# Two-layer encoder trunk: paired token tiles after the mixer, stores issued by POOL, rows reloaded later, an end that runs row by row

## The chip, the cores and the metric

The kernel runs on one core of a Trainium2 chip. Five engines work from streams of their own, each strictly in its own order, and wait for one another by semaphores: TensorE (PE, with its weight loads shown as PEld), VectorE (DVE), ScalarE (ACT), GpSimd (POOL) and SyncE (SP, which here only issues DMAs). The metric is device time in microseconds; less is better.

## What is computed

```python
def _layer_norm(x, g, b): ...          # mean and variance of each row of 1024

def _swiglu(x, w_gate, w_up, w_down):
    g = jnp.einsum('bsd,df->bsf', x, w_gate)
    u = jnp.einsum('bsd,df->bsf', x, w_up)
    return jnp.einsum('bsf,fd->bsd', jax.nn.silu(g) * u, w_down)

def reference(x, ...):
    for layer in range(2):             # layer 0: MLA and sliding window; layer 1: FoX and chunked
        mix = ...                      # attention heads, then one output projection
        x = _layer_norm(DEEPNORM_ALPHA * x + mix, ln1_g[layer], ln1_b[layer])
        ffn = _swiglu(x, ffn_w_gate[layer], ffn_w_up[layer], ffn_w_down[layer])
        x = _layer_norm(DEEPNORM_ALPHA * x + ffn, ln2_g[layer], ln2_b[layer])
    return x
```

x has 1024 tokens of 1024 numbers in float32; the hidden width D_FF is 2816.

## The kernel before

**Precision.** Every float32 operand is split in two fp32r halves: ACT casts the high half (line 105), DVE subtracts to get the low half (line 106), and a product is three matmuls for each 128-deep step (`mm3`, line 127). What is called a split below is this pair of operations. A transposed operand comes from `turn_block`: four 128x128 transposes on PE into one bank of PSUM, then a split out of that bank.

**Stages.** For each layer: the mixer (projections, attention), the late half of the output projection with the first LayerNorm, `gate_up`, `down`, the second LayerNorm. Both FFN products are done by a scheme with seven products of half-size blocks in place of eight (Strassen's), so blocks of the operands are first added to one another.

**Late output projection and LN1.** `out_proj` (line 605) goes over the eight token tiles of 128 rows, 24 matmuls each; DVE adds each half into the row tile (line 619), then `ln_pipe` (line 178) is pushed: statistics on DVE (153, 155), small operations on POOL (144, 146), scale (DVE 193 or 200 with help of ACT 163 and POOL 164), the add of b on DVE (200), the store of the row to `xr_scr` on SP (1269), and `turn_sums` (line 242). For tiles 0 to 3 the row's two halves are transposed at once into the blocks b11 and b21. For tiles 4 to 7 `sums` needs row tt-4 and row tt: it forms four differences t1 to t4 (DVE 252) in two `s` tiles and turns five blocks (PE 235); these are put on a list `later` and run after the last row.

**gate_up** (line 282). 22 steps f (2816 / 128), in pairs. A step is seven products of 12 matmuls, 84 in all, with weights that DVE sums (288, 289) and splits. Its results are combined on DVE and ACT in `t` tiles (365 to 395). The hidden values and their sums, seven to a pair, are stored to HBM (336), as are four sums of the down weights (329), by SP. The first four steps start with one product each, the **heads**, that needs b11 and b21 only (24 matmuls, line 127), and can run while the sums are being made.

**down** (line 420). For each half of the tokens, products over 11 steps j: a1 x b1 and so on, named by their operands (a11·b11, s1·t1, a12·b21, ..., s2·t2, s3·t3, a22·t4), all for four row tiles in four banks. `parts` loads two halves of an operand with SP (430, 431) and splits them (ACT, DVE). The saved rows come back from `xr_scr` (456) and are scaled by ACT (457). Rows 0 to 3 are complete after s2·t2, rows 4 to 7 after a22·t4, the last product; each complete row is pushed into the second LayerNorm, which in layer 0 stores to `x_scr` (SP, 1279) and turns the row for layer 1 (PE 172), and in layer 1 stores the output (1275). s1·t1, s3·t3 and others use the two `pt` banks as accumulators, the same two banks into which `turn_block` turns.

**What sets the order.** The functions are written in program order, several as generators, and a tile framework places each instruction in its engine's stream: program order gives the priority, the pools of tiles (`gp`, `tp` and so on in CFG, number of buffers) decide when a buffer is free. Once placed, each stream is fixed. All DMAs before go out from SP, on one hardware queue.

Of the kernel before, what the change touches and what calls it, by code (L numbers as in the profile page):

```python
# [32 lines left out]
CFG = dict(gp=30, wrp=3, whp=6, sp=3, hp=6, bp=2, tp=11, pd=3, ps=2, pt=2, pv=1)  # L33
# [6 lines left out]
class Core:  # L40
# [137 lines left out]
    def ln_pipe(self, y, g, b, turn, done):  # L178
# [5 lines left out]
        def push(tt):
            if 0 <= tt - 1 < n:
                self.ln_scale(y[tt - 1], st[tt - 1], g)
            if tt < TT:
                st[tt] = self.ln_stats(y[tt])
            if n <= tt < TT:
                mv, r = st[tt]  # L190
                for op, s, row in ((ALU.subtract, mv[:, 0:1], g), (ALU.mult, r, b)):
                    for o in (slice(0, 512), slice(512, D)):
                        nc.vector.scalar_tensor_tensor(y[tt][:, o], y[tt][:, o], s, row[:, o], op0=op,  # L193
                                                       op1=ALU.mult if row is g else ALU.add)
                        if row is b:
                            done(tt, y[tt][:, o], o)
            z = tt - 2
            if 0 <= z < TT:
                if z < n:
                    nc.vector.tensor_tensor(y[z], y[z], b, op=ALU.add)  # L200
                    done(z, y[z])
                if turn is not None:
                    turn(z)
# [78 lines left out]
    def gate_up(self, xb, wgu, ops, later):  # L282
# [3 lines left out]
        heads = 4  # L286
# [30 lines left out]
        def down_sums(j):  # L317
# [103 lines left out]
    def down(self, y, xr_scr, ops, lng, lnb, turn_next, done):  # L421
# [5 lines left out]
        def parts(j, a, b, homes=None):  # L427
# [4 lines left out]
            if homes is None:  # L432
                h, l = (self.w().rearrange("p s c -> p (s c)") for _ in range(2))
            else:
                h, l = next(homes), next(homes)
# [941 lines left out]
```

## Time and profile before

| | us |
|---|---|
| median of 3 runs | 2542.03 (2538.09 to 2548.68) |
| the profiled execution, as timed | 2547.79 |
| its span in the trace | 2546.0 |
| PE busy | 2381.7 (94%) |
| DVE busy | 1657.1 (65%) |
| ACT busy | 1123.6 (44%) |
| POOL busy | 598.0 (23%) |

Stages in the trace: mixer of layer 0 to about 449 us, its late projection and LN1 to 510, gate_up with its heads to 958, down to 1217; the same for layer 1 to 1785, 1870, 2300 and 2524; the last rows are done at 2546. Read first the busy tenths of PE in 40 slices of 63.65 us: where a slice is not at 9, PE is waiting, and the windows, the timeline and the waits of that place say for whom. The granted clock (PEclk) says whether a matmul ran at full speed.

### The profile page before, as it was taken

To read this page: it belongs to the slowest core of one execution; us is meant where nothing else is said; L and a number is where in the kernel's file an instruction comes from. 1 tells how busy PE (TensorE), PEld (TensorE's weight loads), DVE (VectorE), ACT (ScalarE), POOL (GpSimd) and SP (SyncE) were. 2 spreads that over 40 slices of the span, in tenths; PEclk is the share of its full clock that TensorE was granted. 3 is DMA by queue.
4 is the path that set the end of the run, shared out by engine and by line. 5 is a ranking of instruction groups with operands and counts; after the bars stand their busy time and mean duration, and the time that the engine had idled before them with its cause. 6 is when DMAs were issued, how large, how long until landed. Compare 5 with 4: busy or idle time off the path is not lost.

```text
span 2546.0 us, 35845 instructions
## 1 busy us (share of the span) xinstructions
PE 2381.7 (94%) x11912; PEld 1988.3 (78%) x11912; DVE 1657.1 (65%) x3566; ACT 1123.6 (44%) x2292; POOL 598.0 (23%) x966
## 2 busy tenths in 40 slices
PE   8998999889999999969899999999879999999996
PEld 7977887667888887858688888878758788887885
DVE  3577756868677764566546565656768677764567
ACT  5476756342323325334346665554442232324342
POOL 3532455500000000021344654354600000000012
PEclk9999999989999999979899999999979999999998
DMA  4235232325454469314121212141325544459632
GB/s 155 87 101 158 76 112 65 124 83 180 161 162 157 158 231 360 106 61 176 63 79 42 71 44 63 44 147 53 132 80 176 166 154 161 170 169 378 209 110 86
DMA packets 190906, 337.88 MB, mean 133 GB/s; under 512 B 22392, under 2 KB 48376, under 8 KB 190720
## 3 DMA queue, kind: packets, MB, share of 16 engines
q1 hardware_dynamic: 190720, 335.58, 40.1%
q8 instruction: 95, 1.56, 0.3%
q14 instruction: 91, 0.75, 0.1%
HBM read 236.89 MB, written 94.40 MB: 130 GB/s over the span
## 4 chain that ended last, share of the span: by engine, by line
PE 73%; DVE 12%; DMA 7%; ACT 4%; issue 3%; POOL 2%; SPq 1%; DVEq 0%; ACTq 0%; POOLq 0%
PE pd L127 42%; PE ps L127 12%; PE pt L127 7%; PE pv L689 3%; PE pt L678 3%; PE pv L127 2%; DMA wr<-in_wgu 2%; DVE g L106 2%; DMA g<-in_wd 1%; DVE wh L106 1%; DVE s L650 1%; DVE g L200 1%; PE ps L718 1%; DVE g L193 1%; PE ps L719 1%
## 5 line engine op out<-in xcount | busy, mean ns | idle before, releaser
L127 PE MATMUL pd<-g,wh 128*128 128x512 f32 (+1 forms) x2940 | 738.9, 400 | 31.6 <-ACT g L105 8.1
L127 PEld LDWEIGHTS pd<-g,wh 128*128 128x128 f32 (+1 forms) x2940 | 546.7, 190 | 159.0 <-ACT g L105 9.7
L144 POOL TENSOR_SCALAR m<-m 128x1 f32<-128x1 f32 x32 | 16.8, 525 | 1294.8 <-DVE m L155 1293.3
L106 DVE TENSOR_TENSOR wh<-g,wh 128x1024 fp32r<-128x1024 f32 x138 | 173.3, 1260 | 163.7 <-ACT wh L105 148.8
L105 ACT CAST g<-s 128x512 fp32r<-128x512 f32 x192 | 116.7, 621 | 334.7 <-PE pd L127 147.8
L105 ACT CAST wh<-g 128x1024 fp32r<-128x1024 f32 x138 | 145.0, 1053 | 199.6 <-PE pt L127 63.7
L105 ACT CAST h<-pt 128x512 fp32r<-128x512 f32 (+3 forms) x350 | 157.9, 464 | 138.2 <-PE pt L678 122.4
L106 DVE TENSOR_TENSOR h<-pt,h 128x512 fp32r<-128x512 f32 (+2 forms) x334 | 177.5, 538 | 62.9 <-ACT h L105 60.7
L127 PE MATMUL ps<-g,g 128*128 128x512 f32 (+3 forms) x816 | 201.5, 382 | 8.4 <-DMA g<-kr_scr 4.9
L660 POOL TENSOR_SCALAR s<-s,m 128x128 f32<-128x128 f32 (+1 forms) x192 | 138.3, 722 | 232.1 <-DVE m L659 176.9
L127 PEld LDWEIGHTS ps<-g,g 128*128 128x128 f32 x816 | 147.5, 191 | 37.6 <-DVE m L650 7.3
L127 PE MATMUL pd<-g,g 128*128 128x512 f32 (+2 forms) x756 | 174.4, 376 | 2.2 <-ACT g L105 1.1
L116 POOL TENSOR_TENSOR wh<-wr,wh 128x512 fp32r<-128x512 f32 (+4 forms) x113 | 138.8, 1236 | 150.7 <-ACT wh L115 100.6
L655 ACT ACTIVATE s<-s,m 128x128 f32<-128x128 f32 (+1 forms) x192 | 144.1, 751 | 60.5 <-DVE m L653 50.9
L689 PE MATMUL pv<-h,g 128*128 128x256 f32 x928 | 161.6, 295 | 6.2 <-ACT h L105 2.5
L127 PEld LDWEIGHTS pd<-g,g 128*128 128x128 f32 x756 | 137.2, 190 | 26.0 <-ACT g L105 1.9
L127 PE MATMUL pd<-wh,g 128*128 128x256 f32 (+2 forms) x1056 | 154.1, 294 | 0.0
L106 DVE TENSOR_TENSOR g<-s,g 128x512 fp32r<-128x512 f32 x192 | 131.8, 700 | 33.1 <-ACT g L105 31.0
L689 PEld LDWEIGHTS pv<-h,g 128*128 128x128 f32 x928 | 130.0, 190 | 18.4 <-ACT h L105 7.3
L127 PEld LDWEIGHTS pd<-wh,g 128*128 128x128 f32 x1056 | 142.1, 193 | 1.9 <-DVE g L106 0.3
L678 PE MATMUL pt<-ident,s 128*128 128x128 f32 x816 | 134.0, 276 | 7.2 <-POOL s L660 2.7
L127 PE MATMUL pt<-g,g 128*128 128x512 f32 x528 | 135.0, 393 | 3.5 <-DVE t L383 3.0
(235 smaller groups left out, 4388.1 us busy)
## 6 DMA issues: line engine op xcount, KB each, us to landing
wr<-in_wgu SPq DMA_DIRECT2D x192, 256.0 KB, 2.7
g<-in_wd SPq DMA_DIRECT2D x154, 256.0 KB, 4.1
t<-g SPq DMA_DIRECT2D x88, 256.0 KB, 2.0
s<-t SPq DMA_DIRECT2D x88, 256.0 KB, 2.8
g<-s SPq DMA_DIRECT2D x88, 256.0 KB, 4.5
g<-t SPq DMA_DIRECT2D x88, 256.0 KB, 5.2
a<-t SPq DMA_DIRECT2D x66, 256.0 KB, 2.4
g<-a SPq DMA_DIRECT2D x66, 256.0 KB, 5.3
```

What stands on the lines that cost most here:

```text
L105: self.nc.scalar.copy(hi, src)
L106: self.nc.vector.tensor_tensor(lo, src, fv(hi), op=ALU.subtract)
L116: self.nc.gpsimd.tensor_tensor(hl[:, 1, :], raw, fv(hl[:, 0, :]), op=ALU.subtract)
L127: self.nc.tensor.matmul(out, stat[a], mov[c], start=first and i == 0, stop=last and i == 2, skip_group_check=more)
L193: nc.vector.scalar_tensor_tensor(y[tt][:, o], y[tt][:, o], s, row[:, o], op0=op, op1=ALU.mult if row is g else ALU.add)
L200: nc.vector.tensor_tensor(y[z], y[z], b, op=ALU.add)
L650: nc.vector.tensor_tensor_reduce(out=sb[:, x:y], in0=p, in1=in1, scale=1.0, scalar=m0, op0=ALU.add, op1=ALU.max, accum_out=m)
L655: nc.scalar.activation(sb[:, 0:w], sb[:, 0:w], AF.Exp, bias=neg, scale=scale, accum_out=sm)
L660: nc.gpsimd.tensor_scalar(sb[:, 0:w], sb[:, 0:w], rc, 1.0, op0=ALU.mult, op1=ALU.mult)
L678: nc.tensor.transpose(tp[:, (kb - b0) * P : (kb - b0) * P + P], sb[:, (kb - k0) * P : (kb - k0) * P + P], self.ident)
L689: nc.tensor.matmul(pv, vt(kb), pair[kb // 4][l][:, kb % 4, :], start=c == 0, stop=c == 2 * (last + 1 - first) - 1)
L718: nc.tensor.matmul(p, qt[:, q], kt[:, c : c + w], start=True, stop=False)
```

## The change

Six things are done together.

- The late output projection and LN1 take the tiles in the order 0, 4, 1, 5, 2, 6, 3, 7, so that both rows of a pair are there when the second is; `sums` of tiles 4, 5 and 6 run at once, only that of 7 is put off. The differences stand in four `t` tiles in place of two `s` tiles. There are three heads in place of four.
- The stores of gate_up (336, 329), of `xr_scr` and of `x_scr` are issued by POOL in place of SP: 121 in each layer's gate_up, 10 to each `xr_scr`, 10 to `x_scr`, 272 in all. The output's stores stay on SP.
- In `down` the reload of the rows and their scaling stand after the second product instead of the first.
- Rows 0 to 3 are pushed into LN2 after s3·t3 has been written down instead of after s2·t2.
- In the last product seven of eleven j go as in the other products, all four rows for each j; the four j that are left are kept in tiles and run row by row, so that the four rows end 12 matmuls apart.
- Pools: gp 30 to 31, tp 11 to 9; six of the late projection's weights come from the `wh` pool.

```diff
-CFG = dict(gp=30, wrp=3, whp=6, sp=3, hp=6, bp=2, tp=11, pd=3, ps=2, pt=2, pv=1)
+CFG = dict(gp=31, wrp=3, whp=6, sp=3, hp=6, bp=2, tp=9, pd=3, ps=2, pt=2, pv=1)
...
-    def ln_pipe(self, y, g, b, turn, done):
+    def ln_pipe(self, y, g, b, turn, done, order=range(TT)):
...
         def sums(tt):
             a, b = slice(0, 512), slice(512, D)
             x, z = y[tt - 4], y[tt]
-            ta, tb = self.s(), self.s()
-            t1, t2, t3, t4 = ta[:, a], ta[:, b], tb[:, a], tb[:, b]
+            t1, t2, t3, t4 = (self.t() for _ in range(4))
...
                 self.turn_block(xb, "b21", y[tt][:, 512:D], tt)
+            elif tt < TT - 1:
+                sums(tt)
             else:
                 later.append(lambda: sums(tt))
...
-        heads = 4
+        heads = 3
...
             for n, t in ((b11, "t1"), (b12, "t3"), (b22, "t2"), (b21, "t4")):
-                nc.sync.dma_start(o[n], t)
+                nc.gpsimd.dma_start(o[n], t)
...
-            put = lambda n, t: nc.sync.dma_start(o[n], t)
+            put = lambda n, t: nc.gpsimd.dma_start(o[n], t)
...
-        for tt in range(TT):
-            y[tt] = self.g(F32)
-            nc.sync.dma_start(y[tt], xr_scr[tt * P : tt * P + P, :])
-            nc.scalar.mul(y[tt], y[tt], ALPHA)
         us = [self.s() for _ in range(2)]
...
         product(pb, "s1", "t1")
+        for tt in range(TT):
+            y[tt] = self.g(F32)
+            nc.sync.dma_start(y[tt], xr_scr[tt * P : tt * P + P, :])
+            nc.scalar.mul(y[tt], y[tt], ALPHA)
...
             add(y[mt][:, hi], u[mt], y[mt][:, hi])
+        pb = bank_b()
+        kept = 4
+        homes = iter([self.h() for _ in range(6)] + [self.s().bitcast(F32R), self.g()])
+        product(pb, "s3", "t3")
+        last = [parts(j, "a22", "t4", homes) for j in range(n - kept, n)]
+        for mt in range(4):
             push(mt)
-        pb = bank_b()
-        product(pb, "s3", "t3")
         for mt in range(4):
             add(u[mt], pb[mt], u[mt])
...
-        last = [parts(j, "a22", "t4", homes) for j in range(n)]
         pa = bank_a()
+        product(pa, "a22", "t4", m=n - kept)
         for mt in range(4):
-            for j in range(n):
-                mms(pa[mt], last[j], mt, j == 0, j == n - 1)
+            for j in range(kept):
+                mms(pa[mt], last[j], mt, False, j == kept - 1)
             add(y[4 + mt][:, lo], pa[mt], y[4 + mt][:, lo])
             push(4 + mt)
...
-            late_ws.extend(c.out_weights(wo, late, 0, 5, c.g))
+            late_ws.extend(c.out_weights(wo, late, 0, 1, c.g) + c.out_weights(wo, late, 1, 5, c.wflat))
...
+        order = (0, 4, 1, 5, 2, 6, 3, 7)
```

**PE at the end of layer 0's LN1.** Before; line 127 is a matmul (the `pd` tile 6734 is the fourth head), line 235 a transpose of a turn; `s` tiles are sums, `g` tiles rows.

```order
L127 MATMUL pd_6734<-g_6008,wh_6731 128x512
L235 MATMUL pt_6615<-ident,s_6584 128x128 x4
L235 MATMUL pt_6625<-ident,s_6584 128x128 x4
L235 MATMUL pt_6675<-ident,g_4833 128x128 x4
L235 MATMUL pt_6685<-ident,s_6673 128x128 x4
L235 MATMUL pt_6695<-ident,s_6673 128x128 x4
L235 MATMUL pt_6705<-ident,s_6674 128x128 x4
L235 MATMUL pt_6715<-ident,s_6674 128x128 x4
L235 MATMUL pt_6765<-ident,g_4834 128x128 x4
L235 MATMUL pt_6775<-ident,s_6763 128x128 x4
L235 MATMUL pt_6785<-ident,s_6763 128x128 x4
L127 MATMUL pd_6899<-g_6494,g_6822 128x512
```

The same engine and place after the change; line 240 is the turn's transpose, line 130 the matmul, `pd` 6623, 6662 and 6701 are the three heads.

```order
L240 MATMUL pt_6424<-ident,g_4833 128x128 x4
L240 MATMUL pt_6434<-ident,t_6420 128x128 x4
L240 MATMUL pt_6444<-ident,t_6421 128x128 x4
L240 MATMUL pt_6454<-ident,t_6422 128x128 x4
L240 MATMUL pt_6464<-ident,t_6423 128x128 x4
L240 MATMUL pt_6473<-ident,g_4830 128x128 x4
L240 MATMUL pt_6482<-ident,g_4830 128x128 x4
L130 MATMUL pd_6623<-g_5994,wh_6615 128x512
L130 MATMUL pd_6662<-g_5994,wh_6654 128x512
L130 MATMUL pd_6701<-g_5994,wh_6693 128x512
```

Before, ten turns of sums follow the last head; after, all heads follow the turns (sixteen turns stand in a row ahead of them), and of the sums only those of tile 7 come later.

**ACT at the end of layer 0's gate_up.** Before; line 457 scales a reloaded row, 105 is the cast of the next product's operand, 371 and 394 belong to the last step f.

```order
L371 ACTIVATE t_9900<-pd_9859 128x512
L457 ACTIVATE g_10202<-g_10202 128x1024
L457 ACTIVATE g_10205<-g_10205 128x1024
L457 ACTIVATE g_10208<-g_10208 128x1024
L457 ACTIVATE g_10211<-g_10211 128x1024
L457 ACTIVATE g_10214<-g_10214 128x1024
L394 ACTIVATE t_9872<-t_9872 128x512
L457 ACTIVATE g_10217<-g_10217 128x1024
L105 CAST wh_10053<-g_10050 128x1024
```

After; the lines are 377, 400, 108 and 465.

```order
L377 ACTIVATE t_9904<-pd_9863 128x512
L400 ACTIVATE t_9876<-t_9876 128x512
L108 CAST wh_10057<-g_10054 128x1024
L108 CAST wh_10076<-g_10073 128x1024
L108 CAST wh_10095<-g_10092 128x1024
L108 CAST wh_10114<-g_10111 128x1024
L108 CAST wh_10133<-g_10130 128x1024
L108 CAST wh_10152<-g_10149 128x1024
L465 ACTIVATE g_10421<-g_10421 128x1024
L465 ACTIVATE g_10424<-g_10424 128x1024
```

The row scalings have moved from ahead of the operand casts of a11·b11 to behind six more of them.

**PE around s2·t2 and s3·t3 of layer 0.** Before; `pv` 10878 is a bank of s2·t2, line 172 turns rows 0 and 1, `ps` 11200 and 11201 with `pt` 11202 and 11203 are the banks of s3·t3.

```order
L127 MATMUL pv_10878<-wh_11072,wh_11073 128x512
L172 MATMUL pt_11147<-ident,g_10202 128x128 x4
L172 MATMUL pt_11156<-ident,g_10202 128x128 x4
L172 MATMUL pt_11182<-ident,g_10205 128x128 x4
L172 MATMUL pt_11191<-ident,g_10205 128x128 x4
L127 MATMUL ps_11200<-wh_11207 128x512
```

After; `pt` 11103 is a bank of s3·t3, line 175 turns rows 0 to 2, `pd` 11457 is a bank of the last product.

```order
L130 MATMUL pt_11103<-wh_11306,wh_11305 128x512
L130 MATMUL pt_11103<-wh_11305,wh_11306 128x512
L175 MATMUL pt_11394<-ident,g_10421 128x128 x4
L175 MATMUL pt_11403<-ident,g_10421 128x128 x4
L175 MATMUL pt_11427<-ident,g_10424 128x128 x4
L175 MATMUL pt_11436<-ident,g_10424 128x128 x4
L175 MATMUL pt_11622<-ident,g_10427 128x128 x4
L175 MATMUL pt_11631<-ident,g_10427 128x128 x4
L130 MATMUL pd_11457<-wh_11464 128x512
```

The first turns of layer 1's rows stand one product later, and six of them in place of four are in a row.

## Rows read from the trace of the kernel before

**Rows 1.** The page, parts 1 and 2: busy us, share, instructions; busy tenths by slice.

```profile
PE 2381.7 (94%) x11912; PEld 1988.3 (78%) x11912; DVE 1657.1 (65%) x3566; ACT 1123.6 (44%) x2292; POOL 598.0 (23%) x966
...
PE   8998999889999999969899999999879999999996
```

**Rows 2.** Windows: start:end, us, then PE, PEld, DVE, ACT, POOL busy, PEclk, DMA share, GB/s.

```profile
600.00:900.00 300.00, 294.89 (x1291) 243.15 (x1291) 221.96 (x354) 90.81 (x155) 0.00 (x0) 0.99 0.50 162
```

**Rows 3.** Windows around LN1 of layer 0 and of layer 1, columns as in rows 2.

```profile
452.00:506.00 54.00, 46.10 (x202) 36.16 (x201) 48.58 (x82) 18.06 (x32) 30.86 (x26) 0.91 0.36 127
506.00:551.00 45.00, 33.75 (x160) 26.91 (x158) 26.91 (x56) 20.43 (x49) 1.69 (x2) 0.84 0.20 65
...
600.00:650.00 50.00, 44.89 (x188) 36.06 (x188) 37.74 (x61) 12.30 (x21) 0.00 (x0) 0.97 0.58 189
...
1870.00:1900.00 30.00, 20.70 (x102) 16.35 (x101) 18.57 (x42) 13.69 (x36) 0.00 (x0) 0.80 0.06 18
```

**Rows 4.** Groups of PE by line from 506 to 551: busy us, mean ns | idle before.

```profile
L127 PE MATMUL pd<-g,wh 128*128 128x512 f32 x86 | 22.5, 418 | 3.3 <-ACT t L371 2.8 <-ACT t L365 0.6
L235 PE MATMUL pt<-ident,s 128*128 128x128 f32 x56 | 9.9, 327 | 5.5 <-DVE g L106 4.0 <-DVE h L106 1.4
```

**Rows 5.** Timeline of ACT and of PE after gate_up: start, us, operation [idle before <-releaser].

```profile
962.21 1.06 ACT L457 ACTIVATE g<-g 128x1024 f32<-128x1024 f32 x1 [2.00 <-DMA g<-xr_scr]
...
970.39 1.03 ACT L105 CAST wh<-g 128x1024 fp32r<-128x1024 f32 x1
...
971.48 0.97 PE L127 MATMUL pd<-wh 128*128 128x512 f32 x3 [2.12 <-ACT wh L105]
...
2319.55 0.73 PE L127 MATMUL pd<-wh 128*128 128x512 f32 x2 [2.92 <-ACT wh L105]
```

**Rows 6.** Windows at the same two places, columns as in rows 2.

```profile
950.00:975.00 25.00, 21.63 (x88) 16.48 (x87) 12.22 (x16) 14.04 (x16) 0.00 (x0) 0.96 0.91 342
...
2300.00:2325.00 25.00, 20.83 (x82) 15.76 (x81) 13.45 (x17) 14.80 (x17) 0.00 (x0) 0.93 0.95 361
```

**Rows 7.** Timeline of PE around LN2 of layer 0, columns as in rows 5.

```profile
1130.40 1.97 PE L172 MATMUL pt<-ident,g 128*128 128x128 f32 x8 [15.08 <-DVE g L200]
1134.98 1.09 PE L172 MATMUL pt<-ident,g 128*128 128x128 f32 x4 [2.61 <-DVE g L106]
1138.27 1.09 PE L172 MATMUL pt<-ident,g 128*128 128x128 f32 x4 [2.20 <-DVE g L106]
1142.53 1.22 PE L127 MATMUL ps<-wh 128*128 128x512 f32 x2 [3.17 <-ACT wh L105]
```

**Rows 8.** Windows around LN2 of layer 0, columns as in rows 2.

```profile
1100.00:1150.00 50.00, 26.94 (x107) 21.37 (x106) 34.11 (x42) 15.03 (x20) 14.10 (x12) 0.73 0.30 111
1200.00:1250.00 50.00, 40.93 (x169) 29.97 (x168) 28.14 (x47) 12.91 (x27) 19.52 (x20) 0.83 0.24 80
```

**Rows 9.** Timeline of DVE from 1127 and of POOL from 1124, columns as in rows 5.

```profile
1127.00 6.64 DVE L200 TENSOR_TENSOR g<-g,b 128x1024 f32<-128x1024 f32 x2
...
1138.04 1.22 DVE L200 TENSOR_TENSOR g<-g,b 128x1024 f32<-128x1024 f32 x1
1139.17 0.42 DVE L106 TENSOR_TENSOR g<-pt,g 128x256 fp32r<-128x256 f32 x1
...
1124.62 11.23 POOL L164 TENSOR_TENSOR g<-g,b 128x1024 f32<-128x1024 f32 x4
```

**Rows 10.** Timeline of DVE at the end of the kernel, columns as in rows 5.

```profile
2522.94 1.29 DVE L425 TENSOR_TENSOR g<-pd,g 128x512 f32<-128x512 f32 x2 [7.79 <-PE pd L127]
...
2530.11 9.56 DVE L193 SCALAR_TENSOR_TENSOR g<-g,m,b 128x512 f32<-128x512 f32 x8
2539.59 2.35 DVE L200 TENSOR_TENSOR g<-g,b 128x1024 f32<-128x1024 f32 x2
```

**Rows 11.** SP's waits: engine line <- for whom: us, times, longest.

```profile
SPq L329 <- DVE g L289: 107.0, 88, 4.0
...
SPq L1279 <- DVE g L200: 81.3, 3, 79.8
```

More of the change, by code (lines that the diff above doesn't have):

```diff
@@ L182, in ln_pipe, with push @@
         n = TT - 2
[L184 to L190, printed above, removed]
+        at = dict(enumerate(order))
+        def push(i):
+            if 0 <= i - 1 < n:
+                self.ln_scale(y[at[i - 1]], st[i - 1], g)
+            if i < TT:
+                st[i] = self.ln_stats(y[at[i]])
+            if n <= i < TT:
+                mv, r = st[i]
+                yt = y[at[i]]
                 for op, s, row in ((ALU.subtract, mv[:, 0:1], g), (ALU.mult, r, b)):
                     for o in (slice(0, 512), slice(512, D)):
-                        nc.vector.scalar_tensor_tensor(y[tt][:, o], y[tt][:, o], s, row[:, o], op0=op,
+                        nc.vector.scalar_tensor_tensor(yt[:, o], yt[:, o], s, row[:, o], op0=op,
                                                        op1=ALU.mult if row is g else ALU.add)
                         if row is b:
-                            done(tt, y[tt][:, o], o)
-            z = tt - 2
+                            done(at[i], yt[:, o], o)
+            z = i - 2
             if 0 <= z < TT:
                 if z < n:
-                    nc.vector.tensor_tensor(y[z], y[z], b, op=ALU.add)
-                    done(z, y[z])
+                    nc.vector.tensor_tensor(y[at[z]], y[at[z]], b, op=ALU.add)
+                    done(at[z], y[at[z]])
                 if turn is not None:
-                    turn(z)
+                    turn(at[z])
         return push
@@ L431, in parts @@
             nc.sync.dma_start(raw[:, hi], ops[j][b])
[L432 to L435, printed above, removed]
+            h, l = (next(homes) if homes else self.wflat() for _ in range(2))
             self.split(h, l, raw)
@@ L442, in mms, with product @@
             self.mm3(p, (h[:, c], l[:, c]), (h[:, hi], l[:, hi]), first, last, more)
-        def product(p, a, b, first=True):
-            for j in range(n):
+        def product(p, a, b, first=True, m=n):
+            for j in range(m):
                 op = parts(j, a, b)
@@ L595, in out_weights, with out_proj @@
         return ws
-    def out_proj(self, o_scr, x_src, ws, kts, y, push=None, more=None):
+    def out_proj(self, o_scr, x_src, ws, kts, y, push=None, more=None, order=tuple(range(TT))):
         nc = self.nc
         load = lambda tt: self.weight(o_scr[tt, :, kts[0] : kts[-1] + 1, :].rearrange("p k c -> p (k c)"), 512)
-        nxt = load(0)
+        nxt = load(order[0])
         if more is not None:
             ws = ws + more()
-        for tt in range(TT):
-            oh, nxt = nxt, load(tt + 1) if tt + 1 < TT else None
+        for z, tt in enumerate(order):
+            oh, nxt = nxt, load(order[z + 1]) if z + 1 < TT else None
             if x_src is not None:
@@ L1268, in tile_hybrid_trunk @@
         lng, lnb = c.load_row_bcast(ln1g[layer]), c.load_row_bcast(ln1b[layer])
-        push = c.ln_pipe(y, lng, lnb, c.turn_sums(y, xb, later), lambda tt, yt, o=slice(0, D), xr_scr=xr_scr: nc.sync.dma_start(xr_scr[tt * P : tt * P + P, o], yt))
-        drain(c.out_proj(o_scr, None, late_ws, late, y, push, lambda: c.out_weights(wo, late, 5, 8, lambda: c.s().bitcast(F32R))))
+        order = (0, 4, 1, 5, 2, 6, 3, 7)
+        push = c.ln_pipe(y, lng, lnb, c.turn_sums(y, xb, later), lambda tt, yt, o=slice(0, D), xr_scr=xr_scr: nc.gpsimd.dma_start(xr_scr[tt * P : tt * P + P, o], yt), order)
+        drain(c.out_proj(o_scr, None, late_ws, late, y, push, lambda: c.out_weights(wo, late, 5, 8, lambda: c.s().bitcast(F32R)), order))
         push(TT)
@@ L1278, in tile_hybrid_trunk @@
             x_src = scr("x_scr", [S, D])
-            done = lambda tt, yt, o=slice(0, D), x_scr=x_src: nc.sync.dma_start(x_scr[tt * P : tt * P + P, o], yt)
+            done = lambda tt, yt, o=slice(0, D), x_scr=x_src: nc.gpsimd.dma_start(x_scr[tt * P : tt * P + P, o], yt)
             made = []
```

8 lines of the change are left out of this document (3 added, 5 removed).

## The prediction

> **What bounds the kernel now.** I read the shares and the busy tenths first [rows 1]: PE is busy for 94% of the span, and no other engine is near it (DVE 65%). So PE's time is the kernel's time, and an edit can only win where PE stands still. In the steady part of gate_up it does not: from 600 to 900 us PE is busy for 294.89 of 300 us, and DVE has room, 221.96 of 300 [rows 2]. One matmul there costs 294.89 / 1291 = 0.228 us, one step f (84 matmuls) about 19.2 us. The slices that are not at 9 lie at the joints between stages, so I took windows there next, then the timeline of PE for the gap and of the engine that it names. There are four kinds of joints: LN1 of each layer [rows 3, 4], gate_up to down in each layer [rows 5, 6], LN2 of layer 0 [rows 7 to 9], and the end [rows 10]. The change edits all four. What it does not touch (mixers, steady gate_up, the middle of down) I leave at its time.
>
> **LN1, both layers.** From 452 to 506 us DVE is the bound, busy for 48.58 of 54 (90%); from 506 to 551 nobody is: DVE 26.91 and PE 33.75 of 45 [rows 3]. PE there does what is left of the heads and then turns of sums, each of which is a chain of PE, ACT and DVE over two banks: 56 transposes of sums with 5.5 us of waits before them, and the clock at 0.84 [rows 3, 4]. Layer 1 shows the same, 20.70 of 30 at 0.80. The change removes nothing from DVE: its 48.58 + 26.91 = 75.5 us stay. It moves the sums under the stretch that DVE bounds, and the heads behind it. At 100% DVE would be ready for the heads at 452 + 75.5 = 527.5, at the 90% of the earlier stretch at 452 + 84 = 536; I take 532, between them, since more kinds of work are ready. Three heads of 24 x 0.228 = 5.5 us end at 548.5. PE then owes, against 551 before, a fourth head (5.5) and three more turns (3 x 4 transposes of 0.327 [rows 4] = 3.9), so it stands at 557.9, which is 7 behind. Against that, DVE has its sums behind it, and what PE loses later can go: 5.1 us idle from 600 to 650, and a clock of 0.97 there (1.5 us) [rows 3]; from 551 to 600 I put the same clock loss at twice that, 3. With all 9.6 gone the gain is +2.6, with DVE at 527.5 it is +7, with DVE at 536 and none gone -11. I take **+3 a layer, 6 in all** (-22 to +14).
>
> **From gate_up to down, both layers.** ACT works in order, and its first row scaling stands ahead of the casts of a11·b11 and waits for a DMA; the cast that PE needs runs at 970.39 only, and PE waits for 2.12 us in layer 0 and for 2.92 in layer 1 [rows 5]. The windows give 25 - 21.63 = 3.4 and 25 - 20.83 = 4.2 us of idle time, with the DMA engines at 0.91 and 0.95 [rows 6]. The reload moves 8 x 512 KB behind the operands of two products, and the order on ACT shows the casts ahead of the scalings. What is late next is the operand traffic itself: it still has to come. I give back these 7.6 us and a little of the slow clock behind them (0.96 and 0.93): **+8** (+2 to +12). The moved loads stand on SP behind the last operand of s1·t1, which waits for the last step's store, now POOL's. If that were late, scalings are needed one product (132 matmuls, 30 us) later, which covers it.
>
> **LN2 of layer 0.** After s2·t2 PE waits 15.08, 2.61, 2.20 and 3.17 us [rows 7], with 16 transposes in between: rows 0 and 1 have to be normalized first, from the write-down through the statistics, POOL, and the add of b, which takes 6.64 us for two rows since POOL's 11.23 us run beside it [rows 9]. The last 3.17 us come from SP: its store of x_scr stands ahead of the loads of s3·t3 and waits for the same add, 79.8 us the longest [rows 11]. The two windows give 23.1 and 9.1 us idle, with the clock at 0.73 and 0.83 [rows 8]. After the change s3·t3 follows at once and covers the normalization of rows 0 to 3 with 30 us of PE; stores are no longer ahead of loads. A new wait stands behind s3·t3: six turns are placed ahead of the last product, and their two banks are s3·t3's own. They wait for the twelve write-downs (1.29 / 2 = 0.65 us each [rows 10], 7.8 us), then go pair by pair, a low half of 0.42 us each [rows 9] and its ACT half before it: about 13 us until the last product starts, 2.7 of it work at full speed (24 transposes). So 23.1 idle become about 10. At the end of down the rows come 12 x 0.228 = 2.7 us apart and not all at once: of the 9.1 idle I take 5 as left. That is 13 + 4 = 17 us of waits, and some 3 of what the clock of 0.73 over 50 us costs (27 us of matmuls there [rows 8]): **+20** (+8 to +28).
>
> **The end.** PE is done at 2524.3 and the kernel at 2546: four rows end together, and DVE does the rest alone, eight L193 of 9.56 us and two adds, until 2541.94 [rows 10]. From PE's end DVE works 17.6 us for four rows, and the output's store takes 4.1 more. After the change rows end 8.2, 5.5, 2.7 and 0 us before PE's end; the first two are then normalized under matmuls, and half of DVE's work, 8.8 us, is left. With the store and a little for POOL's steps the end moves from 21.7 to about 13.3 us behind PE, +8.4. Against this, the write-downs of s3·t3 now stand on DVE among the operand splits of the last product; of their 7.8 us I let a third stop PE, 2.5. **+6** (+2 to +9).
>
> **Stores by POOL, and the pools.** In gate_up POOL does nothing [rows 2]; in LN1 its 30.86 of 54 us [rows 3] leave room for ten stores. SP loses its waits for results, 107.0 us at line 329 [rows 11], but PE is full there, so that wins nothing by itself. No row shows a store issued by POOL. From below it is nothing; from above, it is POOL's 2.8 us (11.23 / 4) with DVE's add at 3.3 in place of 1.22 beside it [rows 9]. I take nothing: DVE's room is 78 us in 300, some 5 us in each step of 5.5 stores. The `t` pool falls from 11 to 9, and a store that lands later holds its tile longer; the same room of DVE has to cover it.
>
> Here a rule speaks against the change. The Trainium skill, "SBUF — State Buffer", section "SBUF: two separate sides", says that POOL writes the descriptors of its DMAs itself and is locked out while DVE runs certain operations, so that a store of about 620 ns took about 3100. By that a store lands 2.5 us later and the sum stays as it is, unless tiles run short. Its "DMA: Bandwidth & Descriptors", section "Issuing engines are not separate DMA queues", says that issuing from several engines saves only the issuer's time, which fits that I count nothing for the move in gate_up.
>
> **The sum.** 6 + 8 + 20 + 6 = 40 us. The profiled execution took 2547.79 us, its span 2546.0; by the sum it would take 2508. It lies 5.8 us above the median, so on the median's scale 2542 - 40 = **2502**.
>
> **The rivals.**
> *POOL's stores slow the steady part (slower).* Each step f has 5.5 stores. If POOL and DVE block one another for the length of such a store, as line 164 did with DVE's add (2.1 us more for each row of 1024, [rows 9]), DVE loses 5.5 x 2.1 = 11.6 us a step and has 5 [rows 2]: 6.6 us x 44 steps = 290 us, 2790. It decides from 0.9 us a store, and eats the whole gain from 40 / 44 = 0.9 us a step, at 1.1 us a store. For it speaks that every one of the busy DVE operations there reads two operands; against it that a store moves no data through POOL, and that a store's issue is far shorter than 1024 elements. A mild form, a `t` tile that comes 0.5 to 2 us late in each step, gives 22 to 88 us of loss: 2520 to 2590. Chance 0.14, two thirds of it mild.
> *LN1 gains nothing or loses.* DVE is held by the turn chains at 90% or less and the heads, without filler, end late: -11 a layer. Then 8 + 20 + 6 - 22 = 12, 2530. For it: PE has only about 54 us of work in the 80 us ahead of the heads. Chance 0.16.
> *All bounds good.* LN1 +14, gate_up to down +12, LN2 +28, end +9: 63 us, 2479. Chance 0.15.
> *The joints are not shortened as said*, since the operand traffic and the new turns take the place of the old waits: LN2 +8, gate_up to down +2, the rest as above: 22 us, 2520. Chance 0.12.
>
> **How the numbers follow.** The forecast (2492 to 2512) has 0.43. Below 2475 and above 2535 I leave 2 in 10, most of it the slow rival: range 2475 to 2535. A change of 0.5%, 12.7 us, is about what a measurement of this kernel can tell from none. Faster by more than that: 0.43 + 0.15 + 0.12 + most of the LN1 rival + a part of the mild one, 0.82. Same: 0.08. Slower: 0.10.
>
> **What would show it.** Right: from the first head to the 50 us behind it PE is at 9 tenths and the group of transposes of sums has DVE at 90% beside it; no wait of PE for ACT line 108 behind gate_up, and the DMA share there under 0.9; between s2·t2 and s3·t3 no gap, behind s3·t3 one of about 10 us; from PE's last matmul to the end 13 us; a window of 300 us in gate_up still at 295 of PE. Wrong: waits of PE or DVE for `t` tiles in gate_up, DVE's mean there above 0.69 us an addition, heads later than 536.

## The result and the profile after

The changed kernel takes 2568.02 us (median of 4 runs, 2562.83 to 2571.56), the kernel before 2542.28; the ratio is 1.0097, 95% interval 1.0068 to 1.0127. It is slower by 1%, where 2502 was forecast. The profiled run has a span of 2569.0 against 2546.0, 23 us more.

Both kernels issue 11912 matmuls and transposes, stage after stage, so the stages can be compared by the start of the Nth of them (us, worked out from the two traces; inside a stage the order differs, so N stands at the joints). The marks 3200 and 9600 lie some 100 us into gate_up, so what follows from LN1 is counted with it. Each column is one execution: programs that are the same (e6 and e10) or run in the same order (e2 and e15, all below) differ by up to 3.5 and 5.8 us in a stage, so a few us in one stage mean nothing by themselves.

```
N of PE, what ends there       before    after   difference  change in the stage
 2400  mixer, layer 0           449.6    453.3      +3.7        +3.7
 3200  LN1 and heads, layer 0   658.4    671.0     +12.6        +8.9
 4400  gate_up, layer 0         930.4    952.0     +21.6        +9.0
 4800  gate_up to down          1027.2   1044.8    +17.6        -4.0
 5600  down and LN2             1245.0   1246.3     +1.3       -16.3
 8800  mixer, layer 1           1786.1   1781.5     -4.7        -6.0
 9600  LN1 and heads, layer 1   1989.1   1999.9    +10.8       +15.5
11000  gate_up, layer 1         2309.9   2338.5    +28.6       +17.8
11200  gate_up to down          2361.7   2385.4    +23.7        -4.9
11600  down                     2452.4   2476.7    +24.3        +0.6
11911  s3 x t3, last product    2523.9   2554.9    +31.0        +6.7
       end of the span          2546.0   2569.0    +23.0        -8.0
```

The two LN1 lose 24.4 us and the two gate_up 26.8; the three edits of down win 4.0 + 4.9 + 16.3 and, at the end, 8.0 less 6.7. The mixers (+3.7 and -6.0), which the change does not aim at, were not followed up.

**LN1.** The windows of the kernel after that answer to the first two of [rows 3] (columns as there):

```profile
452.00:506.00 54.00, 43.35 (x201) 34.77 (x200) 45.75 (x72) 19.00 (x35) 35.25 (x32) 0.95 0.30 108
506.00:551.00 45.00, 24.04 (x94) 18.68 (x95) 28.96 (x62) 15.58 (x39) 4.43 (x9) 0.57 0.29 94
```

From 506 to 551 PE is busy for 24.04 us in place of 33.75, at a clock of 0.57 in place of 0.84. The stretch is two stretches in one:

```profile
490.00:526.00 36.00, 12.97 (x54) 9.10 (x52) 35.90 (x61) 13.70 (x28) 11.50 (x16) 0.65 0.49 166
526.00:542.00 16.00, 8.53 (x37) 7.06 (x37) 7.16 (x19) 5.99 (x17) 0.00 (x0) 0.50 0.05 21
```

To 526 DVE is the bound and full, 35.90 of 36 us; behind that it has 7.16 us of work in 16, and nobody is full. PE's timeline (start, us, operation [idle before <-releaser]):

```profile
502.23 1.08 PE L240 MATMUL pt<-ident,g 128*128 128x128 f32 x4 [6.86 <-DVE g L109]
508.02 1.08 PE L240 MATMUL pt<-ident,g 128*128 128x128 f32 x4 [4.71 <-DVE g L109]
...
530.58 1.94 PE L240 MATMUL pt<-ident,g 128*128 128x128 f32 x8 [3.20 <-DVE g L109]
533.86 1.94 PE L240 MATMUL pt<-ident,t 128*128 128x128 f32 x8 [1.34 <-DVE g L109]
537.14 1.94 PE L240 MATMUL pt<-ident,t 128*128 128x128 f32 x8 [1.34 <-DVE g L109]
540.38 1.94 PE L240 MATMUL pt<-ident,g 128*128 128x128 f32 x8 [1.30 <-issue]
541.97 9.79 PE L130 MATMUL pd<-g,wh 128*128 128x512 f32 x36
```

Of the sixteen turns the first eight come one by one, as DVE makes their operands and splits; the last eight come two by two, 3.28 us a pair, each pair waiting for a split of the pair before; the first head starts at 541.97. Between the heads of the kernel before a pair took 1.03 us of PE, at full speed; here it takes 1.94:

```profile
534.50 1.03 PE L235 MATMUL pt<-ident,s 128*128 128x128 f32 x8
```

**gate_up.** The steady window of the kernel after in layer 1 (columns as in rows 2):

```profile
1950.00:2300.00 350.00, 335.53 (x1454) 273.76 (x1454) 241.92 (x385) 98.89 (x172) 53.55 (x99) 0.99 0.46 153
```

and of the kernel before:

```profile
1950.00:2250.00 300.00, 297.58 (x1307) 244.46 (x1306) 221.25 (x353) 91.21 (x157) 0.00 (x0) 1.00 0.49 163
```

PE stands still for 14.5 of 350 us, where it lost 2.4 of 300 before. DVE has room as before. The waits of the whole run (engine, line <- for whom: us, times, longest) say for whom, first of PE, then of ACT:

```profile
PE pd L130 <- ACT t L371: 25.1, 18, 3.1
...
ACT g L108 <- DMA t<-g: 31.4, 32, 3.6
```

PE waits for ACT's copy out of a bank (371; 2.4 us in the whole of before, where the copy is line 365), and ACT for a store. ACT's timeline at one such place:

```profile
2085.51 0.62 ACT L108 CAST g<-s 128x512 fp32r<-128x512 f32 x1 [0.25 <-DMA t<-g]
2086.04 0.63 ACT L400 ACTIVATE t<-t 128x512 f32<-128x512 f32 x1
2086.57 0.60 ACT L108 CAST wh<-wr 128x512 fp32r<-128x512 f32 x1
2090.74 0.62 ACT L108 CAST g<-s 128x512 fp32r<-128x512 f32 x1 [3.56 <-DMA t<-g]
2091.27 0.58 ACT L371 COPY t<-pd 128x512 f32<-128x512 f32 x1
```

The cast of a weight into a `g` tile waits 3.56 us until the store of a sum of down weights has read that tile, and the copy that PE needs stands behind it.

**gate_up to down, and LN2.** The joint comes some 22 us later here than before in layer 0 and 29 in layer 1, so these windows, later by about as much, answer to [rows 6]; no row scaling is in them:

```profile
975.00:1000.00 25.00, 23.90 (x103) 18.63 (x102) 15.17 (x19) 8.76 (x11) 3.24 (x6) 1.00 0.93 336
2326.00:2351.00 25.00, 23.91 (x103) 18.67 (x102) 14.50 (x18) 7.39 (x9) 3.24 (x6) 1.00 0.93 345
```

PE is idle for 1.1 us in each, in place of 3.4 and 4.2.

Of [rows 7] these waits of PE are what is left, the first inside s3·t3, the others before the last product:

```profile
1163.35 2.07 PE L130 MATMUL ps<-wh,wh 128*128 128x512 f32 x4 [5.03 <-DVE wh L109]
1172.83 1.25 PE L175 MATMUL pt<-ident,g 128*128 128x128 f32 x8 [1.80 <-DVE s L431]
1178.92 2.28 PE L175 MATMUL pt<-ident,g 128*128 128x128 f32 x8 [4.83 <-DVE g L109]
1181.88 2.29 PE L175 MATMUL pt<-ident,g 128*128 128x128 f32 x8 [0.68 <-DVE g L109]
```

The first was not foreseen, and stands in layer 1 too. DVE and POOL at that place:

```profile
1153.26 6.75 DVE L205 TENSOR_TENSOR g<-g,b 128x1024 f32<-128x1024 f32 x2
1159.94 4.49 DVE L109 TENSOR_TENSOR wh<-g,wh 128x1024 fp32r<-128x1024 f32 x2
...
1149.77 12.44 POOL L167 TENSOR_TENSOR g<-g,b 128x1024 f32<-128x1024 f32 x4
```

This is the picture of [rows 9], moved: two adds take 6.75 us and two splits 4.49 (2.35 otherwise, see e8) while POOL multiplies four rows by g.

**The end.** PE's last matmul starts at 2554.9 and the span ends at 2569.0. DVE's last operations, which answer to [rows 10]:

```profile
2557.01 0.68 DVE L431 TENSOR_TENSOR g<-pv,g 128x512 f32<-128x512 f32 x1
...
2559.97 2.70 DVE L198 SCALAR_TENSOR_TENSOR g<-g,m,b 128x512 f32<-128x512 f32 x2
2562.59 1.21 DVE L205 TENSOR_TENSOR g<-g,b 128x1024 f32<-128x1024 f32 x1
2563.73 1.40 DVE L198 SCALAR_TENSOR_TENSOR g<-g,m,b 128x512 f32<-128x512 f32 x2
```

### The profile page after: what moved, and what is told of

Read it like the earlier page. It is cut to its first block, busy times and chain, and to the rows that moved or that the text cites. A ratio compares the mean times of both kernels' runs of the same rounds, so it can differ in the third digit from the quotient of the medians.

```text
span 2569.0 us, 35947 instructions
## 1 busy us (share of the span) xinstructions
PE 2386.4 (93%) x11912; PEld 1991.0 (78%) x11912; DVE 1662.6 (65%) x3566; ACT 1120.8 (44%) x2292; POOL 746.0 (29%) x1238
## 3 DMA queue, kind: packets, MB, share of 16 engines
q0 software_dynamic: 22912, 76.04, 7.6%
## 4 chain that ended last, share of the span: by engine, by line
PE 56%; issue 23%; DVE 9%; POOL 5%; DMA 4%; ACT 3%; SPq 0%; POOLq 0%; DVEq 0%; ACTq 0%
PE pd L130 33%; PE ps L130 7%; PE pt L130 4%; PE pv L693 3%; PE pt L682 3%; PE pv L130 2%; DVE g L109 1%; DMA wr<-in_wgu 1%; POOL t L335 1%; DVE wh L109 1%; POOL s L342 1%; PE ps L722 1%; PE ps L723 1%; POOL a L342 1%; DVE g L205 1%
## 5 line engine op out<-in xcount | busy, mean ns | idle before, releaser
L130 PE MATMUL pd<-g,wh 128*128 128x512 f32 (+1 forms) x2748 | 699.9, 402 | 46.4 <-ACT t L371 25.1
L130 PEld LDWEIGHTS pd<-g,wh 128*128 128x128 f32 (+1 forms) x2748 | 512.0, 191 | 172.2 <-ACT t L371 33.5
L109 DVE TENSOR_TENSOR wh<-g,wh 128x1024 fp32r<-128x1024 f32 x146 | 181.6, 1251 | 144.2 <-ACT wh L108 123.1
L108 ACT CAST wh<-g 128x1024 fp32r<-128x1024 f32 x146 | 153.1, 1053 | 208.7 <-PE pv L130 87.8
L119 POOL TENSOR_TENSOR wh<-wr,wh 128x512 fp32r<-128x512 f32 (+4 forms) x121 | 149.7, 1244 | 179.4 <-ACT wh L118 136.3
L130 PE MATMUL pd<-wh,wh 128*128 128x512 f32 x672 | 175.8, 395 | 1.1 <-DVE wh L109 1.0
L130 PE MATMUL pd<-g,g 128*128 128x512 f32 (+2 forms) x720 | 161.1, 370 | 0.4 <-DVE g L109 0.3
L342 POOL DMA_DIRECT2D a<-t x66 | 35.7, 541 | 406.8 <-DVE t L397 300.2
L130 PEld LDWEIGHTS pd<-wh,wh 128*128 128x128 f32 x672 | 126.7, 190 | 29.1 <-DVE wh L109 2.8
L130 PEld LDWEIGHTS pd<-g,g 128*128 128x128 f32 x720 | 128.7, 188 | 21.7 <-DVE g L109 1.1
```

Of the source, the lines that this page charges most:

```text
L108: self.nc.scalar.copy(hi, src)
L109: self.nc.vector.tensor_tensor(lo, src, fv(hi), op=ALU.subtract)
L119: self.nc.gpsimd.tensor_tensor(hl[:, 1, :], raw, fv(hl[:, 0, :]), op=ALU.subtract)
L130: self.nc.tensor.matmul(out, stat[a], mov[c], start=first and i == 0, stop=last and i == 2, skip_group_check=more)
L342: put = lambda n, t: nc.gpsimd.dma_start(o[n], t)
```

## The experiments

Times are medians of the runs, each with its ratio to the kernel before on the same chip (2541 to 2545 us).

### e1: stores back on SP

```diff
-                nc.gpsimd.dma_start(o[n], t)
+                nc.sync.dma_start(o[n], t)
...
```

> The changed kernel with all its stores issued by SP again (9 t tiles kept). Against the kernel before the changed one loses, by the time at equal counts of PE's instructions in the two traces, 9 + 19 = 28 us in the two gate_up, 9 + 14 = 23 us in the two LN1, and wins 9 at the reload, 16 at LN2 and 1 at the end. Theory: a store issued by POOL lands later (3.8 against 2.8 us) and frees its t tile later, so ACT's copy, and PE behind it, wait. Then this kernel gets most of the 28 back: about 2542 us. Rival (nine tiles alone are too few, whoever stores): no change, 2565 to 2570.

2559.93 us, ratio 1.0072 (1.0046 to 1.0097). A quarter of the expected gain. Gate_up of layer 1 (9600 to 10800) now loses 3.0 us against before in place of 14.2, and PE waits 9.6 us for the copy in place of 25.1; but 4.9 us of layer 0's gate_up are lost still, and gate_up to down is slower by 3.8 us in place of faster by 4.0. Counted to 11000, the two gate_up lose 7.3 us in place of 26.8. So within gate_up most of the loss does go with POOL's stores, and outside it POOL's stores win. From 1950 to 2300 PE is idle for 3.8 us in place of 14.5:

```profile
1950.00:2300.00 350.00, 346.22 (x1519) 284.10 (x1518) 246.08 (x394) 99.34 (x174) 0.00 (x0) 1.00 0.47 159
```

### e2: pools of before

```diff
-CFG = dict(gp=31, wrp=3, whp=6, sp=3, hp=6, bp=2, tp=9, pd=3, ps=2, pt=2, pv=1)
+CFG = dict(gp=30, wrp=3, whp=6, sp=3, hp=6, bp=2, tp=11, pd=3, ps=2, pt=2, pv=1)
```

> The changed kernel with the pools of before (11 t tiles, 30 g tiles), stores still on POOL. Theory (late stores hold tiles, two more tiles cover that): most of the 28 us in gate_up come back, 2542 to 2550 us, waits of PE for ACT's copy under 5 us in all. Rival (POOL's issues slow DVE or the DMA path itself): no change, 2565 to 2570.

2539.79 us, ratio 1.0000 (0.9989 to 1.0011): all of the loss of gate_up is gone with POOL's stores in place, so with the pools of before POOL's stores cost nothing there. PE's waits for the copy are 7.8 us, not under 5. I put this down to the `t` tiles, as the expectation does; but two pools were changed, and the direct wait is for a `g` tile. One more run decides it:

### e15: only the `g` pool of before

```diff
-CFG = dict(gp=31, wrp=3, whp=6, sp=3, hp=6, bp=2, tp=9, pd=3, ps=2, pt=2, pv=1)
+CFG = dict(gp=30, wrp=3, whp=6, sp=3, hp=6, bp=2, tp=9, pd=3, ps=2, pt=2, pv=1)
```

> The changed kernel with 30 g tiles in place of 31, still 9 t tiles; e2 had changed both pools. In gate_up of the changed kernel the direct wait is ACT's cast into a g tile that a store still reads (31.4 us, 32 times; 15.2 us, 6 times in e2). Theory (the nine t tiles set an order in which that cast stands ahead of PE's copy): no better than the changed kernel, 2565 to 2580 us. Rival (the 31st g tile moves the order): back near e2, 2538 to 2548.

2541.15 us, ratio 0.9986 (0.9977 to 0.9996). My theory falls, the rival holds: with nine `t` tiles and one `g` tile less the kernel is as fast as e2. Every operation on all five engines even stands in the same place as in e2: the two `t` tiles change no order. In this kernel the 31st `g` tile, one more buffer, costs 28 us (0.0111 x 2543). Its steady window in layer 1:

```profile
1950.00:2300.00 350.00, 350.00 (x1546) 289.87 (x1545) 248.59 (x391) 101.78 (x175) 56.24 (x104) 1.00 0.50 171
```

PE is busy for 350 of 350 us. The order of ACT shows why; here is the same step of layer 0's gate_up in both kernels, from the operation 400 of one step to the copy 371 of the next (`t_8104`). With 31 `g` tiles:

```
L400 ACTIVATE t_7963<-t_7963 128x512
L108 CAST wh_8238<-wr_8236 128x512
L108 CAST g_8248<-s_8223 128x512
L371 COPY t_8104<-pd_8091 128x512
```

With 30:

```
L400 ACTIVATE t_7963<-t_7963 128x512
L108 CAST wh_8238<-wr_8236 128x512
L371 COPY t_8104<-pd_8091 128x512
L108 CAST g_8232<-s_8223 128x512
L108 CAST g_8241<-s_8223 128x512
L108 CAST wh_8244<-wr_8221 128x512
L108 CAST g_8248<-s_8223 128x512
```

With one tile more the framework places the casts into `g` tiles ahead of the copy, and one of them meets, on the chip, a tile whose store is not done. With one less it places them behind. ACT's waits for such stores fall from 31.4 us in 32 to 14.1 in 6, PE's for the copy from 25.1 to 8.0.

The order alone is not the whole cause. e1, with 31 `g` tiles and SP's stores, has the same order at this step, and yet PE lost 3.8 us in its window and not 14.5. There ACT waits for stores even longer (108.5 us in 24), but in the steps around 2088 and 2128 us it does so ahead of operation 400 (6.8 and 7.1 us) and not between it and the copy. So the loss needs both, the 31st `g` tile and POOL's stores; why the wait falls elsewhere with SP's stores was not followed further.

### e7: plain order of the tiles

```diff
-        order = (0, 4, 1, 5, 2, 6, 3, 7)
+        order = tuple(range(TT))
```

> The changed kernel with the late projection's tiles in the order 0 to 7 again; the sums of tiles 4, 5 and 6 still follow at once, three heads. Theory: the paired order makes b11 and b21 whole only with the seventh tile, so PE has no heads to do while DVE is the bound, and its clock falls (0.57 from 506 to 551); in plain order the heads fill those gaps and the 23 us of the two LN1 come back: about 2545 us, first head before 510. Rival (sums at once and their chains over two banks are what costs): within 5 us of the changed kernel, 2563 to 2573.

2536.51 us, ratio 0.9976 (0.9964 to 0.9989): 31 us faster than the changed kernel, with sums still at once and three heads. LN1 (2400 to 3200) is at -2.0 us against before in place of +8.9, layer 1's (8800 to 9600) at +2.6 in place of +15.5. Gate_up loses as before it. The first head starts at 491.73 us in place of 541.97, and the clock from 506 to 551 is 0.70 in place of 0.57. The theory holds, though the gain is 8 us more than it said: the two LN1 give 24 of the 31.

### e14: both undone

e2's pools and the plain order together.

> e2 (the changed kernel with 11 t tiles) with the tiles in plain order; sums at once, three heads. It differs from e9 only in these two. Theory (the order costs what it cost at nine tiles, 24 to 31 us, and sums at once nearly nothing): 2508 to 2516 us, and what is left against e9's 2495 is heads and sums. Rival (the order's cost came with the shortage of tiles): 2530 to 2540.

2509.80 us, ratio 0.9868 (0.9853 to 0.9882). By the ratios the order costs 34 us here (30 against e15, whose order is e2's), so it has nothing to do with the pools, and the two causes add up. The theory's other half, that sums at once cost nearly nothing, does not hold: e14 differs from e9, below, in the sums at once and the three heads alone, and is 15 us slower (0.0059 x 2543), 14 of them in the two LN1 (-4.7 against -13.1, -0.1 against -6.1). Sums and heads were not taken apart.

### e6: the three edits of down alone

The changed kernel with stores on SP, pools 30 and 11, and these lines. The `t` tiles for the differences and the late projection's weights from `wh` (four of them, not six) are still in it.

```diff
-        order = (0, 4, 1, 5, 2, 6, 3, 7)
+        order = tuple(range(TT))
-            elif tt < TT - 1:
-                sums(tt)
-        heads = 3
+        heads = 4
```

> Of the change only the three edits of the down stage are left (reload after the second product, rows 0 to 3 pushed after s3 x t3, last product's end row by row), with the sums' differences in t tiles; stores on SP, 11 t tiles, plain order, four heads, sums last. Theory (costs and gains add up place by place): 2542 - 9 - 16 - 1 = 2516 us, gate_up and LN1 as before. Rival (the gains at down need the stores off SP, since SP's store of x_scr stood ahead of the loads): LN2 of layer 0 loses half of its 16, about 2525.

2519.08 us, ratio 0.9918 (0.9898 to 0.9938), as the theory said. LN2 (4800 to 5600) is at -18.3, so it needs no stores off SP. PE's 5.03 us stop in both layers is there too.

### e9: POOL's stores where nothing else is short

e6 with all stores on POOL.

> e6_down_only (11 t tiles, plain order) with all stores on POOL. Theory (a late store costs only where tiles run short): within 5 us of e6, 2514 to 2524. Rival (POOL's stores slow gate_up whatever the number of tiles): 2530 or more.

2495.37 us, ratio 0.9809 (0.9794 to 0.9825), 28 us less than e6 by the ratios (0.0109 x 2543) and 23 less than e10, which is e6's program again, on the chip of e9. Neither theory nor rival: the stores on POOL are a gain. By the table's marks the two LN1 win 10 and 6 us (2400 to 3200: -13.1 against -2.9; 8800 to 9600: -6.1 against 0), layer 0's gate_up 5, of which 3.5 are scatter (e6 +5.4, e10 +1.9 there). From 452 to 506, e6 first, then e9:

```profile
452.00:506.00 54.00, 47.75 (x209) 37.77 (x208) 47.66 (x79) 19.39 (x34) 34.03 (x28) 0.91 0.37 133
```

```profile
452.00:506.00 54.00, 50.12 (x233) 39.63 (x232) 49.02 (x81) 22.64 (x40) 37.14 (x36) 1.00 0.40 135
```

24 more of PE's operations are done in the same 54 us, at a clock of 1.00 in place of 0.91. The move also changed the order: between 400 and 600 us PE, ACT and DVE do part of their work in another order in e9 than in e6, so the gain is that of the move with its order.

### e13: only the stores of rows on POOL

e9 with line 335 and 342 on SP again.

> e9 with the stores of gate_up (242) on SP again; those of xr_scr and x_scr (30) stay on POOL. By the time at equal counts of PE's instructions e9 wins over e6 10 and 6 us in the two LN1 and 5 us in layer 0's gate_up. Theory (in LN1 the stores of rows stood on SP ahead of the loads of the heads' weights, and this is what POOL relieves): LN1 stays as in e9, 2500 to 2504 us. Rival (gate_up's stores are what counts, in the first steps too): near e6, 2515 to 2520.

2508.50 us, ratio 0.9866 (0.9850 to 0.9883): halfway. The 30 stores of rows win some 8 to 13 us (against e10 and e6), the 242 of gate_up some 14. LN1 of layer 0 keeps 9.9 of its 13.1, that of layer 1 only 2.1 of 6.1. In e6 SP waits for 27.1 us at the stores of rows (line 1272) between 440 and 530 us, and of the loads of gate_up's weights (297) behind them the tenth to thirteenth go out at 508.7 to 515.5; in e9 these waits are gone, the loads go out at 502.8 to 509.5, and in e9 and e13 the first 72 matmuls of heads are done some 10 us sooner than in e6 (513.6 and 515.0 against 524.4). That the loads are what the heads waited for is likely, not shown.

### e11: the fourth of the square

The changed kernel, 11 `t` and 30 `g` tiles, stores on SP.

> The changed kernel with 11 t tiles and with its stores on SP: the fourth of a square with the changed kernel (POOL, 9: 2568), e1 (SP, 9: 2560), e2 (POOL, 11: 2540). Theory (late stores matter only where tiles are short): as e2, 2537 to 2543 us. Rival (effects add): 2540 - 8 = 2532 us.

2546.91 us, ratio 1.0007 (0.9996 to 1.0019), against 1.0000 with the stores on POOL. The time lies above the range, but so does that of the kernel before on this chip (2545 against 2541); by the ratios, whose intervals overlap, it is as e2, as the theory said, and the rival falls. So POOL's stores are 6 us worse than SP's with 31 `g` tiles, no different with 30, and 23 to 28 better in the form of e6 and e9. The last two differ in the order, the sums and the heads; why the gain is in one alone is open.

### e8: the multiplication by g on DVE

```diff
-        nc.gpsimd.tensor_tensor(y, y, g, op=ALU.mult)
+        (eng or nc.gpsimd).tensor_tensor(y, y, g, op=ALU.mult)
```

In LN2 `eng` is DVE for rows 0 to 3; the rest is e6.

> e6_down_only with the multiplication by g of rows 0 to 3 in LN2 (line 167) on DVE in place of POOL. In e6 PE stops for 5.03 us in s3 x t3 of each layer, for DVE's splits; DVE's adds beside POOL's line 167 took 6.76 us for two and its splits 4.49 for two. Theory (POOL and DVE block one another): DVE does four more operations of 1.2 us but its adds and splits are at 1.2 each again, the gap of 5.03 goes or falls under 2 in both layers: 2519 - 8 = 2511 us. Rival (the gap is DVE's own order, rows ahead of splits): the four added operations lengthen it to 7 or more, 2519 to 2525.

2507.78 us, ratio 0.9855 (0.9841 to 0.9870), 16 us less than e6 by the ratios and 11 less than e10, e6's program on this chip. By the marks 6.5 us less than in e6 are spent in down and LN2 of layer 0, and 6.6 less behind 11600. DVE at the place:

```profile
1131.74 1.22 DVE L205 TENSOR_TENSOR g<-g,b 128x1024 f32<-128x1024 f32 x1
1132.88 1.22 DVE L109 TENSOR_TENSOR wh<-g,wh 128x1024 fp32r<-128x1024 f32 x1
1134.02 1.22 DVE L205 TENSOR_TENSOR g<-g,b 128x1024 f32<-128x1024 f32 x1
1135.15 2.35 DVE L167 TENSOR_TENSOR g<-g,b 128x1024 f32<-128x1024 f32 x2
1137.42 2.35 DVE L109 TENSOR_TENSOR wh<-g,wh 128x1024 fp32r<-128x1024 f32 x2
```

and PE's wait in s3·t3:

```profile
1138.69 1.20 PE L130 MATMUL ps<-wh,wh 128*128 128x512 f32 x4 [0.37 <-DVE wh L109]
```

DVE has four operations more and is done earlier: every one is at 1.2 us again, and 5.03 became 0.37. The theory holds.

### e10: rows of layer 1 pushed where they were

```diff
+        if turn_next is None:
+            for mt in range(4):
+                push(mt)
         pb = bank_b()
...
-        for mt in range(4):
+        for mt in range(4 if turn_next is not None else 0):
             push(mt)
```

> e6_down_only with rows 0 to 3 of layer 1 pushed after s2 x t2 as before; in layer 0 they stay after s3 x t3. Theory: the row work that now stands on DVE among the splits of s3 x t3 and of the last product is what costs 6.8 us in layer 1's down (11600th to last matmul), as nothing of layer 1 is turned, so the move wins nothing there: 2519 - 5 = 2514 us. Rival (the cost comes from the last product's own new form): no change.

2518.36 us, ratio 0.9898 (0.9876 to 0.9919), whose interval overlaps e6's. The two waits of 5.03 us remain, but the run says nothing about them: on all five engines every operation stands in the same place as in e6. The framework placed the pushed rows where they were, so the edit changed only the text of the program, and the run is e6 measured again. The difference of the two, 5 us by the ratios, is scatter. That the wait comes from POOL's multiplication beside the splits is shown by e8; the rival's cause, the new form of the last product, falls there too, since e8 keeps that form and has lost the 6.8 us.

### e12: the best of it

e9 with e8's multiplication.

> e9 (three edits of the down stage, all stores on POOL, 11 t tiles, plain order, four heads, sums last) with e8's multiplication by g of rows 0 to 3 in LN2 on DVE. Theory (two independent causes): 2495 - 11 = 2484 us, no wait of 5.03 in s3 x t3. Rival (with stores on POOL the multiplication's place is taken by the stores): 2492 or more.

2482.94 us, ratio 0.9762 (0.9748 to 0.9777): 61 us faster than the kernel before, 85 faster than the change. The wait of 5.03 us is 0.37. It keeps the three edits of down and the stores on POOL, and leaves out the paired order, the sums at once, the three heads in place of four and the other pools.

## Why the prediction was wrong, step by step

**What bounds the kernel**: right. PE is the kernel's time, and everything was decided at PE's gaps.

**LN1**: +6 forecast, -24.4 measured. The step that failed is the start of the heads: "At 100% DVE would be ready for the heads at 452 + 75.5 = 527.5, at the 90% of the earlier stretch at 452 + 84 = 536; I take 532". The first head came at 541.97. DVE was the bound as said, and even at 100%, but only to 526. Eight of the sixteen turns were left then, and they ran in the chain over two banks: 16 us, in which DVE was busy for 7.16. The sum spread all of DVE's work over one stretch at one pace and gave those turns no time of their own. I had named that chain as what is slow before the change, and then priced the stretch as if DVE alone bounded it. The three heads then ended at 566.5 and not at 548.5: they took 24.5 us in place of 16.5, with 2.70 and 1.16 of waits for ACT's copy and their first matmuls still at the lower clock. The clock made it worse, since PE had little to do: from 506 to 542 it was granted 0.50, the lower of its two levels (1.2 GHz), after gaps of 6.86 and 4.71 us, so the transposes took twice as long. The later idle time did go as said (600 to 650 us is full), but that pays for 9.6 us only. The rival "LN1 gains nothing or loses", -11 a layer with 0.16, had this part right; measured 8.9 and 15.5. That the order is a cause is shown (e7, e14: 31 and 34 us); the sums at once and the three heads cost another 15 (e14 against e9).

**The pools**: one sentence, cost nothing; measured 26.8 us in the two gate_up. The step that failed is "a store that lands later holds its tile longer; the same room of DVE has to cover it": what met the late store was ACT, which works in order, at a `g` tile, with PE's copy behind it. I looked at the pool that shrank (11 to 9) and not at the one that grew, since one buffer more cannot make a tile scarcer. e15 shows that it can cost: it moves the order. And it costs this much only together with POOL's stores: 7.3 us of the 26.8 are left with SP's (e1). The mild form of the slow rival, a `t` tile late in each step, gave 22 to 88 us. The size came true, and in part the kind (the copy into a `t` tile was late, 25.1 us in 18 waits), but not the cause: no `t` tile was late for want of tiles, as e15 with nine of them shows. The order of ACT in gate_up was there to be read ahead of the prediction; the three orders that I showed lay elsewhere.

**POOL's stores**: nothing taken. In the form of e6 and e9 they win 23 to 28 us, a third to a half of it with the stores of rows. Those to `xr_scr` the prediction did not price; the stores of gate_up it put aside because "PE is full there". That is so in steady gate_up (e9 and e13 differ by 0.4 us from 3200 to 4400), but not in LN1 and the first steps behind it, where e13 loses 3.3 and 4.0 us against e9. A store on POOL did land later, by 1.0 us, where the prediction named 2.5. The Trainium skill, "SBUF — State Buffer", section "SBUF: two separate sides", has that figure for a `tensor_copy` on DVE beside the DMA, and says of `tensor_tensor`, which is what DVE runs in gate_up, that it did not stall a DMA. The DMA issues of lines 335 and 342 in the changed kernel (names, count, KB each, median us to landing):

```profile
t<-g POOLq DMA_DIRECT2D x88, 256.0 KB, 3.0
s<-t POOLq DMA_DIRECT2D x88, 256.0 KB, 3.8
```

From SP before they took 2.0 and 2.8. The strong form of the rival, POOL's stores slowing DVE, is refuted: DVE's additions in steady gate_up stay at 0.69 us.

**gate_up to down**: +8 forecast, 8.9 measured; right in what went, though the DMA share stayed at 0.93, not under 0.9 as I said it must be.

**LN2**: +20 forecast, 16.3 measured. Right in what went and what came: of the 10 us of waits forecast before the last product, 1.80 and then 5.5 came. The stores need not leave SP for it (e6: -18.3 with stores on SP). The wait of 5.03 in s3·t3 was missed: I let PE's 30 us cover the rows' work and did not ask what POOL's multiplications would meet there.

**The end**: +6 forecast, 1.3 measured. The tail shrank by 8.0 (8.4 forecast). The cost was 6.7 in place of 2.5, and not the write-downs: nearly all of it goes in e8 (11600 to the last matmul is +0.2 there against before, +6.8 in e6), so it is POOL's multiplication again.

## What to carry to other kernels

A buffer more can be an edit of the order: where a scheduler places instructions by when tiles come free, read the order of the in-order engines in the fullest stage after any change of a pool. When waits are gathered in one place, price that place by the chain that is left without its filler, not by the busiest engine's sum; here PE's clock fell on top. Before an edit of the program text is called tested, see that an engine's order has changed (e10). And when work is moved under another stage, ask what it shares there with what is on the path: POOL's multiplication beside DVE's adds and splits cost both.

## What the runs showed of the hardware

- POOL's multiplication of 1024 numbers a row and DVE's operations on two operands hold one another up: four of POOL's took 12.44 us, two adds 6.75 in place of 2.35, two splits 4.49 in place of 2.35, and with POOL out of it DVE did its adds, splits and multiplications at 1.2 us each (e8). The Trainium skill, "SBUF — State Buffer", section "SBUF: two separate sides", says that a pair of ports is held by one of the two at a time; e8 agrees, though no run shows the ports themselves.
- A store issued by POOL keeps POOL busy for 0.54 us and goes out on a queue of its own (q0, 22912 packets, 76.04 MB); stores that waited for no result were issued 0.73 us apart.
- Transposes behind short gaps ran at half speed for tens of microseconds: eight took 1.94 us in place of 1.03, with a granted clock of 0.50 from 506 to 542 us, while PE was busy for 15 of 36 us.
